# Gated pairs that take turns, retention states in one bank, and pauses in front of transpositions, in a two-layer hybrid decoder

## The chip, the cores and the metric

The kernel runs on one core of a Trainium2 chip. The metric is the device time of one execution in microseconds. The engines are named as the profile does: PE is TensorE (PEld its weight loads), DVE is VectorE, ACT is ScalarE, POOL is GpSimd, and SP issues the loads.

## What is computed

Two layers over 528 tokens (16 learned ones and 512 of the input) of width 1024, everything in float32. Each layer has a mixer and a gated feed-forward part. The mixer makes one projection to 3600 columns; four heads of retention and four heads of gated linear attention (GLA) work on it, and one output projection of 1024 columns follows. Cut to what matters here:

```python
def _mixer(h, pos, w_in, ...):
    rq, rk, rv, rg, gq, gk, gv, gr, ga = jnp.split(h @ w_in, offs, axis=-1)
    # retention: rotary on rq and rk, scores with a fixed decay per head, a state carried from chunk to chunk
    o_ret = _head_group_norm(_retention(rq, rk, rv), ret_norm_w) * silu(rg)
    # GLA: the decay of each key column is computed from the data (ga), a state carried likewise
    log_a = log_sigmoid(ga @ gla_gate_w2 + gla_gate_b) / GLA_TAU
    o_gla = _head_rms_norm(_gla(gq, gk, gv, log_a), gla_norm_w) * silu(gr)
    return jnp.concatenate([o_ret, o_gla], axis=-1) @ w_out

def _conv_ffn(h, ffn_up, ffn_conv_w, ffn_conv_b, ffn_down):
    u = h @ ffn_up                      # 2 x 2816 columns
    conv = ...                          # causal, depthwise, width 3
    a, g = jnp.split(conv, 2, axis=-1)
    return (gelu(a) * g) @ ffn_down

for i in range(2):
    h = h + _rmsnorm(_mixer(_rmsnorm(h, ...)), ...)
    h = h + _rmsnorm(_conv_ffn(_rmsnorm(h, ...)), ...)
```

## The kernel before

**Products.** Activations are kept transposed, with the 1024 columns on eight groups of 128 partitions and the 528 tokens along the free axis. Each float32 product is made of three float16 ones (`product_step`, L410 to L412): high part times high part, high times low, low times high. Weights come in blocks of 128 columns (`Block`), loaded by SP and split by ACT (L110) and DVE (L111) into a `unit`. A projection of one block is made in two halves of the tokens (232 and 296), 24 matmuls each, into the PSUM tile `pj`; its evacuation follows on ACT or, for the rotary heads, in `rope`.

**Work in the background.** The mixer's loop walks over the 29 blocks. After each half projection it calls `advance`, which gives one credit to each of two queues of Python generators and steps them while they have credit: `gated` holds the two GLA pairs (heads 0, 1 and heads 2, 3), `bg` all else. A plain step costs 0.6 of a credit, a step of a GLA level `LEVEL` of it. A generator that yields "waits" lets the next in its queue try. `pause(n)` yields "waits" until n further half projections have been made. So a generator's step decides where in program order its instructions come. The program order is a priority: a planner that knows estimated costs then orders each engine's instructions, and each engine keeps that order on the chip. The exception are parts marked to stay in program order. At the end of the mixer `drain` runs both queues until they are empty.

**GLA.** `gla(pr)` makes the decay (`gla_decay`), then `gla_scores`: a diagonal part and seven levels. At each level ACT and DVE write keys and queries as float16 pairs (`lvx`, L885 and L886), POOL and DVE multiply them by the decay for the level after (L888, L890), and in the following step `level_scores` makes the products (`lps`, L836), which DVE copies under a mask (L841 to L849). Then come `k_natural` (transpositions), `gla_states` (`kv`, L788 to L792) and, in a generator of its own in `bg`, `head_out`. In the queue `gated`, pair 0 is stepped to its end before pair 1.

**Retention.** `ret(hd)`: `ret_scores`, `k_natural`, `ret_states` (L775 and L776), `head_out`. In `ret_states` the four chunks are added up in one 128x128 part of a PSUM bank, which is copied after each:

```python
        ps = self.mx([P, P], "kv")
        for c in range(4):
            nc.tensor.matmul(ps, kn[:, c, :], vn(c), start=c == 0, stop=True, skip_group_check=c > 0)
            nc.scalar.activation(sn[:, c, :], ps, AF.Copy)
```

**Values and outputs.** `vtr` waits one half projection and transposes the values (`v_natural`, tile `ptv`). `head_out` multiplies scores and states with them (tile `o`, L694 to L701), normalises (retention: L712, L713, L724 on DVE; GLA: squares L719 and scaling L726 on ACT; the inverse roots on POOL, L344), waits for the gate, transposes the result (tile `pto`, L736), multiplies it by the gate (L739) and splits it into `merged` (L348, L349), from which the output projection (`po`) is made. All these PSUM tiles but those of the projections come from a pool of five banks (`mx`).

**Last feed-forward part.** In layer 1 the gated activations are written in quarters (`quarters`) for a product that needs seven products of quarter size in place of eight. Sums and early quarters lie in one tile `fk` for all eleven column groups.

## Time and profile before

| | |
|---|---|
| median of 3 runs | 1273.32 us (1272.81 to 1274.58) |
| the profiled execution | 1272.69 us, its span 1270.9 us |
| granted clock of PE, mean | 0.995 |
| busy: PE, PEld, DVE, ACT, POOL | 1236.3, 1018.6, 804.1, 666.0, 156.8 us |
| first matmul of the output projection, layer 0 and 1 | 244.51 us, 880.48 us |
| quarters' product in layer 1 | from 1159.40 us |

Times in the profile are counted from the span's start. The busy time of PE is that of overlapping matmuls with modelled ends, so it can be near the span while matmuls run slower than they might. The granted clock is the share of full speed that PE was given. In a row of a group, the numbers behind the first bar are busy time and mean nanoseconds of one; behind the second stands the idle time of the engine just before them, with what ended most of it. A wait goes by "who waited <- who released it".

### The profile page before, as it was taken

How to read it: one execution, taken by the hardware profiler on the slowest of the kernel's cores; microseconds unless marked ns; L12 is line 12 of the kernel's file. 1: busy time of each engine (PE TensorE's matmuls, PEld its weight loads, DVE VectorE, ACT ScalarE, POOL GpSimd, SP SyncE). 2: the span in 40 equal slices, each digit the busy share in tenths (PEclk: the TensorE clock that was granted, in tenths of full speed). 3: DMA queues.
4: the chain of work that ended last, by engine and by line, in shares of the span. 5: the costliest groups of instructions: out<-in, count | busy, mean ns of one | idle time of the engine just before them, and what ended most of it. 6: DMA issues, size and time to landing. Idle time of an engine off the chain costs nothing.

```text
span 1270.9 us, 26355 instructions
## 1 busy us (share of the span) xinstructions
PE 1236.3 (97%) x11106; PEld 1018.6 (80%) x11106; DVE 804.1 (63%) x1390; ACT 666.0 (52%) x1318; POOL 156.8 (12%) x206
## 2 busy tenths in 40 slices
PE   8999899999999999999999998999999999999997
PEld 7778678888788888888887786788898888886443
DVE  5584573557876666613286845735478867887677
ACT  5664554454855555523256645444547656664442
POOL 1021130044000000000141211310430000000001
PEclk9999999999999999999999999999999999999999
DMA  7832112222433333315142321122215333304471
GB/s 214 255 103 76 51 52 67 68 68 66 133 101 100 101 92 92 92 47 131 31 137 67 101 84 51 51 68 68 84 51 150 106 103 102 123 1 159 147 246 70
DMA packets 206827, 124.18 MB, mean 98 GB/s; under 512 B 6688, under 2 KB 194132, under 8 KB 206708
## 3 DMA queue, kind: packets, MB, share of 16 engines
q1 hardware_dynamic: 206548, 121.97, 32.4%
q8 instruction: 87, 1.43, 0.5%
q0 software_dynamic: 160, 0.52, 0.1%
q14 instruction: 32, 0.26, 0.1%
HBM read 120.38 MB, written 2.10 MB: 96 GB/s over the span
## 4 chain that ended last, share of the span: by engine, by line
PE 88%; DVE 5%; ACT 5%; POOL 1%; issue 1%; POOLq 0%; DVEq 0%; ACTq 0%
PE pu L411 12%; PE pu L412 12%; PE pu L410 12%; PE pl L1166 8%; PE pj L410 7%; PE pj L411 7%; PE pj L412 7%; PE pd L411 3%; PE pd L412 3%; PE pd L410 3%; PE po L411 2%; PE po L410 2%; PE po L412 2%; DVE unit L111 1%; ACT unit L110 1%; PE o L694 1%
## 5 line engine op out<-in xcount | busy, mean ns | idle before, releaser
L411 PE MATMUL pu<-every,unit 128*128 128x296 f16 (+2 forms) x1408 | 385.4, 274 | 2.1 <-DVE every L349 2.1
L412 PE MATMUL pu<-every,unit 128*128 128x296 f16 (+2 forms) x1408 | 385.4, 274 | 0.0
L410 PE MATMUL pu<-every,unit 128*128 128x296 f16 (+2 forms) x1408 | 383.7, 274 | 0.7 <-ACT every L348 0.7
L111 DVE SCALAR_TENSOR_TENSOR unit<-st,unit 128x1024 f16<-128x1024 f32 x184 | 229.1, 1246 | 191.1 <-ACT unit L110 190.6
L410 PEld LDWEIGHTS <-unit 128*128 128x128 f16 x2912 | 285.9, 98 | 50.6 <-issue 6.9
L412 PEld LDWEIGHTS <-unit 128*128 128x128 f16 x2912 | 285.8, 98 | 46.8 <-issue 3.1
L411 PEld LDWEIGHTS <-unit 128*128 128x128 f16 x2912 | 286.1, 98 | 42.6 <-issue 0.6
L110 ACT ACTIVATE unit<-st 128x1024 f16<-128x1024 f32 x184 | 191.4, 1041 | 121.3 <-PE pu L412 52.7
L410 PE MATMUL pj<-every,unit 128*128 128x296 f16 (+2 forms) x896 | 248.8, 278 | 1.3 <-DVE room L849 0.7
L412 PE MATMUL pj<-every,unit 128*128 128x296 f16 (+2 forms) x896 | 248.4, 278 | 0.7 <-DVE unit L111 0.7
L411 PE MATMUL pj<-every,unit 128*128 128x296 f16 (+2 forms) x896 | 248.5, 278 | 0.0
L1051 ACT ACTIVATE u<-pu 128x296 f32<-128x296 f32 (+2 forms) x176 | 66.4, 379 | 94.9 <-PE pu L412 94.8
L412 PE MATMUL pd<-av,unit 128*128 128x232 f16 (+1 forms) x352 | 96.9, 276 | 0.0
L411 PE MATMUL pd<-av,unit 128*128 128x296 f16 (+1 forms) x352 | 96.8, 276 | 0.0
L410 PE MATMUL pd<-av,unit 128*128 128x232 f16 (+1 forms) x352 | 96.7, 276 | 0.0
L376 DVE TENSOR_TENSOR acc<-acc,sq 128x296 f32<-128x296 f32 (+2 forms) x60 | 33.4, 558 | 81.5 <-ACT sq L374 79.6
L344 POOL TENSOR_TENSOR every<-every 128x1 f32<-128x1 f32 (+5 forms) x33 | 38.9, 1181 | 337.9 <-DVE every L343 169.5
L1166 PE MATMUL pl<-unit,fk 128*128 128x512 f16 x330 | 71.4, 379 | 0.0
L1040 DVE SCALAR_TENSOR_TENSOR cg<-u,every,cg 128x527 f32<-128x527 f32 (+1 forms) x88 | 66.7, 758 | 5.4 <-ACT cg L1035 4.3
L412 PE MATMUL po<-merged,unit 128*128 128x296 f16 (+2 forms) x256 | 70.0, 274 | 0.0
L411 PE MATMUL po<-merged,unit 128*128 128x296 f16 (+2 forms) x256 | 70.0, 274 | 0.0
L410 PE MATMUL po<-merged,unit 128*128 128x296 f16 (+2 forms) x256 | 69.6, 274 | 0.0
(224 smaller groups left out, 1515.7 us busy)
## 6 DMA issues: line engine op xcount, KB each, us to landing
st<-in_ffn_up SPq DMA_DIRECT2D x88, 512.0 KB, 3.7
st<-in_w_in SPq DMA_DIRECT2D x56, 512.0 KB, 4.5
st<-in_ffn_down SPq DMA_DIRECT2D x46, 512.0 KB, 3.8
st<-in_w_out SPq DMA_DIRECT2D x16, 512.0 KB, 3.5
st<-in_ffn_down SPq DMA_DIRECT2D x8, 384.0 KB, 3.0
out<-yo SPq DMA_DIRECT2D x8, 256.0 KB, 2.0
xt<-in_x SPq DMA_DIRECT2D x6, 256.0 KB, 6.5
w<-in_ffn_down SPq DMA_DIRECT2D x3, 512.0 KB
```

Of the source, the lines that this page charges most:

```text
L110: nc.scalar.activation(u[:, 0], st, AF.Copy, scale=SW)
L111: nc.vector.scalar_tensor_tensor(out=u[:, 1], in0=st, scalar=SW, in1=u[:, 0], op0=ALU.mult, op1=ALU.subtract)
L344: nc.gpsimd.tensor_tensor(out=r[:w, :n], in0=t[:w, :n], in1=self.mhalf[:w, :n], op=ALU.pow)
L376: eng.tensor_tensor(out=acc[:, :n], in0=acc[:, :n], in1=sq[:, :n], op=ALU.add)
L410: nc.tensor.matmul(ps[:, :n], w[:, 0, kk, :], x[:, 0, n0:n1], start=first, stop=False)
L411: nc.tensor.matmul(ps[:, :n], w[:, 0, kk, :], x[:, 1, n0:n1], start=False, stop=False)
L412: nc.tensor.matmul(ps[:, :n], w[:, 1, kk, :], x[:, 0, n0:n1], start=False, stop=last)
L694: nc.tensor.matmul(o[:, i, :], intra(i), vn(i), start=i == 0, stop=i == 0, skip_group_check=i > 0)
L1040: nc.vector.scalar_tensor_tensor(out=to, in0=u[:, max(lo, d) - d : L - d], scalar=self.cvec[:, ci(i) : ci(i) + 1], in1=to, op0=ALU.mult, o ...
L1051: nc.scalar.activation(u[:, n0:n1], ps[:, : n1 - n0], AF.Copy, scale=IXW)
L1166: mm = lambda x, w, **kw: nc.tensor.matmul(ps, x, w, skip_group_check=more, **kw)
```

## The change

There are five parts:

- Pairs: in the queue `gated` a generator that made a step goes to the end of the queue, so the two pairs alternate. `LEVEL` goes from 1.5 to 1.7. The ring of small value tiles `vnt` has eight places instead of six.
- Retention states: the four products go to four parts of one bank; ACT copies the first, DVE adds the others one after another. All is one step with a pause of two behind it.
- GLA states: one step instead of two, with a pause of two behind it and one of one in front.
- Pauses: two instead of one in front of `v_natural`, one in front of the retention states, two between normalisation and transpositions in `head_out`. There the two halves of a head come in one step instead of two. `drain` now counts beats, so that pauses end in it.
- The tile `fk` becomes eleven tiles, one for each column group.

```diff
-LEVEL = 1.5
+LEVEL = 1.7
...
-MIXKINDS = (("vnt", P, 6), ("mv", 10, 4), ...
+MIXKINDS = (("vnt", P, 8), ("mv", 10, 4), ...
...
                 if n != "waits":
+                    if queue is self.gated:
+                        queue.append(queue.pop(i))
                     return n or 1.0
...
     def drain(self):
         while self.bg or self.gated:
+            self.beat += 1
...
     def head_out(self, heads):
...
+        yield
+        yield from self.pause(2)
         for (on, ont), (*_, wcol, gate, slot, _) in zip(onvs, heads):
             while gate[0] is None:
                 yield "waits"
             merged = self.merged[slot] = self.g([P, 2, L], F16, "merged")
             for t0, t1, n0, n1 in [(0, 2, 0, HALF), (2, 5, HALF, L)]:
-                yield
                 pt = self.mx([P, WN], "pto")
...
                 self.split(merged, t[:, :w], n0, n1)
+            yield
...
     def ret_states(self, kn, vn, res):
-        ps = self.mx([P, P], "kv")
+        ps = self.mx([P, 4, P], "kv")
         for c in range(4):
-            nc.tensor.matmul(ps, kn[:, c, :], vn(c), start=c == 0, stop=True, skip_group_check=c > 0)
-            nc.scalar.activation(sn[:, c, :], ps, AF.Copy)
-            if c % 2:
-                yield
+            nc.tensor.matmul(ps[:, c, :], kn[:, c, :], vn(c), start=True, stop=True)
+        nc.scalar.activation(sn[:, 0, :], ps[:, 0, :], AF.Copy)
+        for c in range(1, 4):
+            nc.vector.tensor_tensor(out=sn[:, c, :], in0=sn[:, c - 1, :], in1=ps[:, c, :], op=ALU.add)
+        yield from self.pause(2)
...
     def gla_states(self, kn, tot, vn, res):
         nc.scalar.activation(sn[:, 0, :], ps[:, 0, :], AF.Copy)
-        yield
         for c in range(1, 4):
             nc.vector.scalar_tensor_tensor(out=sn[:, c, :], ...)
-        yield
+        yield from self.pause(2)
...
         def gla(pr):
             heads = (2 * pr, 2 * pr + 1)
+            yield from self.pause()
...
         def ret(hd):
             while ("rv", hd) not in vnat:
                 yield "waits"
+            yield from self.pause()
             yield from self.ret_states(res["kn"], vnat["rv", hd], res)
...
         def vtr(key):
-            yield from self.pause()
+            yield from self.pause(2)
...
         def quarters(col, ca, cg):
             if col == 0:
-                f = cell(self.keep, [P, 5, HK, HT], F32, "fk", "fk", 1)
...
             if col < HK:
-                f = keep["f"][:, j]
+                t = cell(self.keep, [P, 5 * HT], F32, "fk", "fk", HK)
+                f = t[:, : 3 * HT].rearrange("p (n t) -> p n t", n=3)
+                keep["f"].append(f)
+                keep["early"].append(...)
+                keep["sums"].append(...)
```

More of the change, by code (lines that the diff above doesn't have):

```diff
@@ L67 @@
 KINDS = (("rs_t", 10, 4), ("rs_r", 10, 4), ("sst", 1, 4))
-MIXKINDS = (("vnt", P, 6), ("mv", 10, 4), ("bst", 6, 8), ("ms", 10, 4), ("ont", P, 8), ("dgrt", 16, 4), ("dgt", 32, 2))
+MIXKINDS = (("vnt", P, 8), ("mv", 10, 4), ("bst", 6, 8), ("ms", 10, 4), ("ont", P, 8), ("dgrt", 16, 4), ("dgt", 32, 2))
 def cell(pool, shape, dt, tag, name, bufs=None):
@@ L1062, in quarters @@
             if col == 0:
-                f = cell(self.keep, [P, 5, HK, HT], F32, "fk", "fk", 1)
-                view = lambda t, n: t.rearrange("p n j t -> p (n j t)").rearrange("p (j n t) -> p j n t", j=HK, n=n)
-                keep.update(f=view(f[:, :3], 3), early=view(f[:, 3:].bitcast(F16), 4))
-                keep["sums"] = keep["f"].rearrange("p j n t -> p j (n t)").bitcast(F16).rearrange("p j (i n t) -> p j i n t", i=2, n=3)
-            if col == HK:
-                keep["late"] = self.room.bitcast(F16)[:, : HK * 4 * HT].rearrange("p (j n t) -> p j n t", j=HK, n=4)
-            if col < HK:
-                f = keep["f"][:, j]
+                keep["late"] = self.room.bitcast(F16)[:, : HK * 4 * HT].rearrange("p (j i n t) -> p j i n t", j=HK, i=2, n=2)
+                keep.update(f=[], early=[], sums=[])
+            if col < HK:
+                t = cell(self.keep, [P, 5 * HT], F32, "fk", "fk", HK)
+                f = t[:, : 3 * HT].rearrange("p (n t) -> p n t", n=3)
+                keep["f"].append(f)
+                keep["early"].append(t[:, 3 * HT :].bitcast(F16).rearrange("p (i n t) -> p i n t", i=2, n=2))
+                keep["sums"].append(t[:, : 3 * HT].bitcast(F16).rearrange("p (i n t) -> p i n t", i=2, n=3))
                 nc.vector.scalar_tensor_tensor(out=f[:, 0::2], in0=halves(ca), scalar=SA, in1=halves(cg), op0=ALU.mult, op1=ALU.mult)
@@ L1074, in quarters @@
             else:
-                f, e = cell(self.keep, [P, 5, HT], F32, "kl", "kl", 2), keep["f"][:, j]
+                f, e = cell(self.keep, [P, 5, HT], F32, "kl", "kl", 2), keep["f"][j]
                 nc.vector.scalar_tensor_tensor(out=f[:, :2], in0=halves(ca), scalar=SA, in1=halves(cg), op0=ALU.mult, op1=ALU.mult)
@@ L1081, in quarters @@
             for src, names, to in groups:
-                t = keep[to][:, j] if to == "sums" else keep[to][:, j].rearrange("p (i n) t -> p i n t", i=2)
+                t = keep[to][:, j] if to == "late" else keep[to][j]
                 nc.scalar.activation(t[:, 0], src, AF.Copy)
```

## The prediction

> **What bounds the kernel now.** I read the page first, then the stages, then what TensorE (PE) waited for, then the places where its clock fell. The page's span, busy shares and chain by engine:

> ```profile
> span 1270.9 us, 26355 instructions
> PE 1236.3 (97%) x11106; PEld 1018.6 (80%) x11106; DVE 804.1 (63%) x1390; ACT 666.0 (52%) x1318; POOL 156.8 (12%) x206
> PE 88%; DVE 5%; ACT 5%; POOL 1%; issue 1%; POOLq 0%; DVEq 0%; ACTq 0%
> ```

> PE sets the end: 88% of the chain. The number of its matmuls does not change, so only time in which PE waits or runs at a lower clock can be won. Where that is, the busy time by stage shows (stretch, its length, then PE, PEld, DVE, ACT, POOL busy, granted clock, DMA share, GB/s):

> ```profile
> 120.00:180.00 60.00, 55.24 (x588) 43.65 (x587) 40.55 (x108) 34.51 (x90) 15.54 (x17) 0.97 0.18 54
> 180.00:245.00 65.00, 64.27 (x583) 54.51 (x582) 28.68 (x72) 28.76 (x88) 5.50 (x5) 1.00 0.23 66
> 750.00:810.00 60.00, 54.03 (x555) 43.05 (x555) 37.27 (x101) 32.50 (x88) 12.59 (x17) 0.94 0.18 53
> 810.00:880.00 70.00, 69.33 (x667) 58.98 (x660) 34.02 (x84) 31.93 (x93) 8.44 (x14) 1.00 0.24 69
> 1110.00:1140.00 30.00, 30.00 (x274) 25.97 (x273) 25.49 (x37) 18.06 (x30) 0.00 (x0) 1.00 0.01 2
> ```

> The mixers lose 4.8 and 6.0 us in their middle, at 120:180 and 750:810, also with a lower clock; in the stretches after those PE lacks only 0.7 us each. The last feed-forward part (1110:1140) is full. The waits of PE, by who released it (total, times, longest):

> ```profile
> PE lps L836 <- ACT lvx L885: 2.4, 3, 1.1
> PE kv L775 <- ACT sn L776: 1.6, 3, 0.9
> PE pto L736 <- DVE on L724: 1.4, 2, 0.7
> PE ptv L661 <- ACT gv L923: 1.4, 1, 1.4
> PE lps L836 <- DVE lvx L886: 1.4, 3, 0.7
> PE pto L736 <- DVE tmp L739: 1.2, 2, 0.6
> PE pto L736 <- DVE room L849: 1.1, 2, 0.5
> PE kv L775 <- ACT room L670: 0.9, 2, 0.5
> PE lps L836 <- ACT merged L348: 0.7, 1, 0.7
> PE ptv L662 <- ACT vn L669: 0.6, 2, 0.3
> PE lps L836 <- DVE tmp L739: 0.4, 1, 0.4
> ```

> These are what the edits aim at: level scores (lps) whose operand was just being made, states (kv) alternating with ScalarE's copies, transpositions (pto, ptv) issued right behind what they transpose. One such place, in order of time (start, duration, instruction, in brackets the idle time before):

> ```profile
> 155.52 0.41 PE L736 MATMUL pto<-every,on 128*128 128x128 f32 x2 [0.54 <-DVE room L849]
> 155.82 0.91 DVE L739 SCALAR_TENSOR_TENSOR tmp<-pto,every,gr 128x256 f32<-128x256 f32 x2
> 156.62 1.38 DVE L724 TENSOR_SCALAR on<-o,room,every 128x128 f32<-128x128 f32 x4
> 156.78 0.19 PE L836 MATMUL lps<-lvx 64*128 64x64 f16 x1 [0.44 <-DVE tmp L739]
> 158.05 0.46 PE L736 MATMUL pto<-every,on 128*128 128x128 f32 x2 [0.72 <-DVE on L724]
> ```

> Outputs of a gated pair, normalisation of a retention head and a level meet on VectorE (DVE), and PE, which keeps its order, waits 1.7 us in three pieces. What follows such a place, in stretches of 3.4 us (columns as above):

> ```profile
> 155.10:158.50 3.40, 1.76 (x10) 0.93 (x10) 3.40 (x12) 0.84 (x2) 0.87 (x1) 0.98 0.00 0
> 158.50:161.90 3.40, 3.40 (x16) 2.15 (x16) 3.40 (x10) 1.86 (x5) 1.79 (x2) 0.52 0.00 0
> 790.00:793.40 3.40, 1.64 (x10) 1.05 (x10) 3.40 (x13) 0.84 (x2) 0.82 (x1) 0.97 0.02 4
> 793.40:796.80 3.40, 3.40 (x16) 2.10 (x17) 3.40 (x10) 1.90 (x5) 1.90 (x2) 0.52 0.02 5
> 803.40:806.80 3.40, 3.40 (x21) 2.73 (x19) 3.40 (x11) 2.40 (x4) 0.68 (x2) 0.51 0.03 7
> 702.00:705.40 3.40, 1.58 (x12) 1.13 (x13) 2.43 (x5) 1.24 (x2) 0.00 (x0) 1.00 0.23 66
> ```

> After a stretch with PE busy for about half, 3.4 us run at half clock: three times, each worth 3.4 x (1 - 0.52) = 1.6 us, 4.9 in all. It is no sure consequence: 702.0 was as empty and the clock stayed.

> **The change, part by part.** I count places in slots, one after each half projection (0 to 57 in a layer), by following the credits: 1 per slot, a plain step costs 0.6, a level 1.5 before and 1.7 after.

> *Turns and LEVEL.* Before, pair 0 has its levels at slots 15, 16, 18, 19, 21, 22, 24, 25 and pair 1 at 31 to 42. After, pair 0 at 17, 21, 24, 27, 31, 34, 38, 41 and pair 1 at 19, 22, 26, 29, 33, 36, 39, 43. The density is nearly the same, but between the preparation of a level and its scores lie 3.3 slots instead of 1.5. That should end the waits of lps for lvx: 2.4 + 1.4 = 3.8 us. Instructions: none added. Moved: pair 0's states from slot 27 to 47 and the products of its output from 30 to 49, and its output transpositions from 33-35 to 52. So the place at 155 us loses one of its three parties, and the late stretch (180:245), where DVE has 36 us free of 65, gets it. More tiles live at once (my count: 26 instead of 20 of 41 slots), so nothing waits for a slot. The longer ring of small v tiles (8 for 6) is needed, because the first gated one is now held to slot 49 and the seventh is made at 45: no wait either. No DMA is issued by the moved steps, so SP's queue keeps its order; POOL's powers and level products move with their steps and POOL is busy 5.5 of 65 us there.

> *Retention states.* Four products go into four parts of a bank instead of one that is copied and added to in turn, one copy and three adds follow. The prices come from these groups:

> ```profile
> L776 ACT ACTIVATE sn<-kv 128x128 f32<-128x128 f32 x32 | 8.8, 274 | 28.6 <-PE kv L775 28.6
> L792 DVE SCALAR_TENSOR_TENSOR sn<-sn,tots,kv 128x128 f32<-128x128 f32 x12 | 4.1, 345 | 12.0 <-ACT sn L789 11.8
> ```

> ```profile
> DVE sn L792 <- ACT sn L789: 11.8, 4, 3.0
> ```

> Over 8 heads ACT loses 24 x 0.274 = 6.6 us, DVE gains 24 adds; the form (a plain add from PSUM) is not in the trace, its nearest is L792, so 24 x 0.345 = 8.3 us. Both lie beside PE: DVE is 63% busy. PE's wait for the copies, 1.6 us, goes. A new wait is DVE's for the first copy: the same step of the gated pairs has DVE wait 11.8 us in four, 3.0 at most, so at most 8 x 3.0 = 24 us, behind which rope and weight splits queue. No wait row of PE names those four, so I take 0; the pause of two slots behind the adds (48 matmuls) covers their 0.27 + 3 x 0.35 = 1.3 us. If the cover goes, it is 1.3 x 8 = 10 us, the other end; below zero it cannot go by more than the 1.6 already counted.

> *Pauses.* A pause is no wait on the chip: it moves the step one or two slots back in program order. In front of v transpositions and states it should take the 1.4 (ptv behind gv) and the 0.9 (kv behind L670). In front of output transpositions: 1.4 + 1.1, and the 0.7 and 0.4 that level scores waited in the same crowd, 3.6 in all. I leave standing 1.2 (pto behind tmp) and 0.6 (ptv behind vn): those wait for a PSUM bank, and the two halves of a head are now issued in one step, which helps no bank. Who waits for a later output? The output projection alone, whose last operand is the head of the last gate (slot 57) before and after.

> *Eleven tiles.* The same operations on the same number of bytes, in separate tiles. The largest of them:

> ```profile
> L1084 DVE TENSOR_TENSOR fk<-kl,fk 128x768 f16<-128x768 f32 x11 | 10.5, 956 | 6.4 <-ACT fk L1083 6.4
> ```

> PE is full there and DVE has 4.5 of 30 us free. The cost lies between 0 and one such split that comes late, 1.0 us; a gain is excluded, since PE has nothing to win in 1110:1140. I take 0. The added beat in the last drain only lets pauses end.

> *Sum.* Waits 3.8 + 1.6 + 1.4 + 0.9 + 3.6 = 11.3. Clock: the three crowds thin out, but 702.0 shows that it hangs on more than the filling; I take two of three, 3.3. Against it, new waits in slots 44 to 57, where both pairs' states and outputs now lie together: between 0 and what states and outputs cost today (1.6 + 1.4 + 0.9 + 3.6 = 7.5); I take the middle, 4, since the free DVE speaks for less and the doubled halves for more. 11.3 + 3.3 - 4 = 10.6. The profiled execution took 1272.69, so 1262.1; the median of the runs stands 0.6 above it: 1263.

> [...]

> **The rivals.**
> (E) More comes back than I count: all three clock stretches, no new wait, and the refill behind each wait. The flow of matmuls shows the refill:

> ```profile
> 130.20 0.26 PE L412 MATMUL pj<-every,unit 128*128 128x232 f16 x1
> 130.30 0.26 PE L410 MATMUL pj<-every,unit 128*128 128x232 f16 x1
> ```

> They start 0.10 apart and last 0.26, so a wait loses 0.16 beyond its bracket; 18 waits make 2.9. 11.3 + 4.9 + 2.9 = 19.1: 1254.

> (B) The waits only move. The planner orders PE by its own estimates, and every reshuffle has places where they are wrong. Then only the 1.6 of the states and little else goes: 1271. For it: the waits sit at different places in the two layers. Against: the releasers are the same few, and all get more distance.

> [...]

> (D) Slower: PSUM banks. Five banks serve all but the projections; a pair's output takes four from its products until it is scaled. Its rows:

> ```profile
> L726 ACT ACTIVATE on<-o,every 128x128 f32<-128x128 f32 x32 | 8.9, 356 | 2.2 <-POOL every L344 2.2
> L719 ACT ACTIVATE on<-o 128x128 f32<-128x128 f32 x32 | 8.3, 276 | 19.0 <-PE o L699 19.0
> L719 ACT ACTIVATION_READ_ACCUMULATOR on<-o 128x1 f32 x32 | 6.7, 208 | 0.0
> L344 POOL TENSOR_TENSOR every<-every 128x1 f32<-128x1 f32 (+5 forms) x33 | 38.9, 1181 | 337.9 <-DVE every L343 169.5
> ```

> Ten squares of 0.276 + 0.208, a power of 1.2, ten scalings of 0.356: 9.6 us. The pairs now come at slots 49 and 50, and retention heads between. If PE waits out one pair's hold in each layer, 19.2, and one clock stretch each, 3.2, against 11.3 + 3.3 gained, it is 7.8 slower: 1281. It decides from 7.3 us of such waits a layer. For it: bank waits exist (1.2, 0.6). Against: slots 44 to 57 hold fourteen half projections that the planner can put in between, and pair 1's output there costs PE almost nothing today (0.7 us idle in 180:245).

> **How the numbers follow.** Forecast 0.60 (1257 to 1269, 1263 its middle), E 0.10, B 0.12, C 0.06, D 0.12. The range leaves out D and the slow end of C: 1253 to 1275. About 0.2%, 2.5 us, is what a measurement of this kernel tells from no change. Faster: forecast, E and a twentieth of the rest, 0.75; same: B and part of C, 0.12; slower: D and the rest of C, 0.13.

> **What would show it.** Level scores with no wait for lvx; kv with no wait for sn; PE fuller in 120:180 and 750:810 and the clock at 1.00 there; in the late stretches more DVE and ACT work, and up to 4 us of waits of pto and o. The last feed-forward part unchanged. Wrong it would be if those late stretches lose more than they did in the middle, or if half clock appears behind the transpositions at slots 47 to 55.

## The result, and the profile after

The changed kernel takes 1250.37 us (median of 4 runs, 1250.15 to 1251.25) against 1273.28 us for the kernel before: a ratio of 0.982, with an interval of 0.9803 to 0.9837. It is 22.9 us faster, more than twice the forecast of 10.3 and below the low end of the range. Its profiled execution has a span of 1248.4 us, 22.5 less.

Page and chain of the changed kernel:

```profile
span 1248.4 us, 26366 instructions
PE 1227.0 (98%) x11106; PEld 1017.4 (81%) x11106; DVE 806.5 (65%) x1414; ACT 654.2 (52%) x1290; POOL 157.1 (13%) x206
PE 92%; DVE 3%; POOL 2%; ACT 1%; issue 1%; DVEq 0%; POOLq 0%; ACTq 0%
```

As many matmuls as before, 24 instructions more on DVE and 28 fewer on ACT. 24 of these are copies of the states. The other four are ACT_TABLE_LOADs of 1.28 us each, which I had not foreseen: the decays of both pairs now run in turns, and each of two lines has one load in a layer where it had two (groups of the kernel before, then of the changed one):

```profile
L819 ACT ACT_TABLE_LOAD x4 | 5.1, 1283 | 0.1
L923 ACT ACT_TABLE_LOAD x4 | 5.1, 1283 | 0.1
```

```profile
L824 ACT ACT_TABLE_LOAD x2 | 2.6, 1283 | 0.0
L928 ACT ACT_TABLE_LOAD x2 | 2.6, 1283 | 0.0
```

PE is a still larger part of the chain. The stages that answer to those shown of before (stretch, length, PE, PEld, DVE, ACT, POOL busy, clock, DMA share, GB/s):

```profile
120.00:180.00 60.00, 60.00 (x693) 51.59 (x692) 38.69 (x100) 26.99 (x55) 12.48 (x16) 1.00 0.28 80
180.00:236.00 56.00, 55.33 (x488) 46.56 (x486) 28.02 (x82) 28.66 (x107) 6.24 (x4) 1.00 0.17 48
740.00:800.00 60.00, 60.00 (x720) 51.30 (x719) 40.35 (x104) 26.76 (x55) 13.69 (x23) 1.00 0.25 73
800.00:858.00 58.00, 57.37 (x509) 48.17 (x507) 27.77 (x81) 29.91 (x109) 6.51 (x8) 1.00 0.19 55
1090.00:1120.00 30.00, 30.00 (x278) 26.25 (x276) 25.55 (x36) 19.02 (x31) 0.00 (x0) 1.00 0.01 1
```

The middle of both mixers is full, where 4.8 and 6.0 us were missing, and the clock is 1.00. In the late stretches PE lacks 0.7 and 0.6 us, no more than before, though both pairs' states and outputs now lie there. The last feed-forward part is unchanged. The stretch in which PE was busy for 1.76 of 3.40 us before is full now, with the same DVE at its limit:

```profile
155.10:158.50 3.40, 3.40 (x51) 2.77 (x49) 3.40 (x7) 1.06 (x1) 2.07 (x3) 1.00 0.34 101
```

What is left of PE's waits in the mixers, but for 0.8 us of pj in front of the levels (total, times, longest):

```profile
PE pto L740 <- DVE on L727: 1.0, 2, 0.7
PE d L871 <- DVE dg L873: 0.9, 1, 0.9
PE ptv L665 <- DVE dg L873: 0.6, 1, 0.6
PE pto L740 <- DVE tmp L743: 0.3, 1, 0.3
```

No lps and no kv is in the list. The slack has changed sides: now DVE sits idle for 16.1 us until level scores come, 8 times; before, that was 2.5 us in 3 (first row of the changed kernel, second of the kernel before, from what the users of the tile lps waited for):

```profile
  PE lps L841: 16.1, 8
  PE lps L836: 2.5, 3
```

By the first matmul of each stage, the 22.5 us split as follows: layer 0 from the gate logits (z) to the first product of the output projection took 205.9 us and takes 195.7; layer 1 from the first projection to there, 226.5 and 213.0; the opening, which the change does not touch, is 1.2 us longer (over all profiles of this document the first gate logits come between 38.6 and 40.3 us); all the rest is the same within 0.2. So 10.1 and 13.5 come from the two mixers and from nowhere else.

### The profile page after: what moved, and what is told of

It reads as the page before. It is cut to its first block, busy times and chain, and to the rows that moved or that the text cites. A ratio compares the mean times of both kernels' runs of the same rounds, so it can differ in the third digit from the quotient of the medians.

```text
span 1248.4 us, 26366 instructions
## 1 busy us (share of the span) xinstructions
PE 1227.0 (98%) x11106; PEld 1017.4 (81%) x11106; DVE 806.5 (65%) x1414; ACT 654.2 (52%) x1290; POOL 157.1 (13%) x206
## 4 chain that ended last, share of the span: by engine, by line
PE 92%; DVE 3%; POOL 2%; ACT 1%; issue 1%; DVEq 0%; POOLq 0%; ACTq 0%
PE pu L414 12%; PE pu L415 12%; PE pu L413 12%; PE pl L1173 8%; PE pj L413 8%; PE pj L415 7%; PE pj L414 7%; PE pd L413 3%; PE pd L414 3%; PE pd L415 3%; PE po L413 2%; PE po L415 2%; PE po L414 2%; PE lps L841 1%; DVE unit L111 1%
## 5 line engine op out<-in xcount | busy, mean ns | idle before, releaser
L111 DVE SCALAR_TENSOR_TENSOR unit<-st,unit 128x1024 f16<-128x1024 f32 x184 | 227.1, 1234 | 162.0 <-ACT unit L110 156.3
L347 POOL TENSOR_TENSOR every<-every 128x1 f32<-128x1 f32 (+5 forms) x33 | 38.9, 1181 | 289.2 <-DVE every L346 192.0
```

The source lines that it names most:

```text
L111: nc.vector.scalar_tensor_tensor(out=u[:, 1], in0=st, scalar=SW, in1=u[:, 0], op0=ALU.mult, op1=ALU.subtract)
L347: nc.gpsimd.tensor_tensor(out=r[:w, :n], in0=t[:w, :n], in1=self.mhalf[:w, :n], op=ALU.pow)
```

## The experiments

Twelve kernels ran, each five rounds or more against the kernel before on the same chip; numbers are ratios to that. e1 to e4 shared one chip, e5 to e8 a second, e9 to e12 a third. The changed kernel itself has 0.982 in the result and 0.9801 as e9 and did not run beside e5 to e8, so distances to it are given for both. I began with three theories. Theory 1, distance: each wait of PE costs its bracket, a refill and now and then 3.4 us at half clock, and the parts take waits away by putting steps farther behind their operands. Theory 2, place: the gain is that pair 0's output leaves the crowded middle. Theory 3: a lucky reshuffle. After the first four runs I added theory 4: the parts need one another.

**Each part alone.** e1 has the turns:

```diff
-LEVEL = 1.5
+LEVEL = 1.7
-... ("vnt", P, 6) ...
+... ("vnt", P, 8) ...
...
                 if n != "waits":
+                    if queue is self.gated:
+                        queue.append(queue.pop(i))
```

> The kernel before with the turns, LEVEL 1.7 and the longer ring of small value tiles alone. Theory 1 (distance: a wait of PE costs its bracket, a refill and now and then 3.4 us at half clock; turns take the waits of lps for lvx, 3.8 us, the pair's part in the crowds at 155 and 790, 2.2 us, two or three clock stretches, 3.3 to 4.9, and refills, 2): 11 to 13 us faster than before, about 1261. Theory 2 (place: nearly all of the gain comes from moving pair 0's output out of the crowded middle): 18 us or more faster, 1255 or less. Theory 3 (a lucky reshuffle of the planner's order, parts do not add): between 3 faster and 3 slower, with new waits at other places.

Measured: 0.996 (0.9948 to 0.9973), 5 us, less than half of what I expected. The waits of lps for lvx are gone, as I had said, but others came (PE's waits in e1):

```profile
PE kv L777 <- ACT vn L671: 2.5, 2, 1.2
PE pto L738 <- ACT on L728: 2.3, 3, 1.9
PE lps L838 <- DVE on L726: 2.2, 2, 1.1
PE ptv L663 <- ACT gv L925: 2.0, 1, 2.0
```

All but one are behind ACT. And the clock fell where it had not before, at the end of layer 1 (stages of e1):

```profile
858.00:862.00 4.00, 1.87 (x13) 1.11 (x12) 0.83 (x2) 2.02 (x9) 2.00 (x2) 1.00 0.44 131
862.00:866.00 4.00, 4.00 (x17) 3.20 (x18) 3.56 (x10) 2.67 (x10) 0.11 (x1) 0.54 0.02 4
866.00:870.00 4.00, 4.00 (x17) 3.55 (x18) 0.44 (x1) 1.46 (x9) 0.00 (x0) 0.50 0.00 0
870.00:874.00 4.00, 4.00 (x20) 2.23 (x20) 0.17 (x1) 1.84 (x13) 0.79 (x1) 0.50 0.01 2
874.00:878.00 4.00, 4.00 (x29) 2.92 (x27) 0.00 (x0) 0.64 (x2) 1.16 (x1) 0.76 0.00 0
```

This stretch of half clock lasts 13.7 us, and 6.8 are lost. The profiled run took 1270.78 us; six of the twelve runs of e1 take 1266.2 to 1267.4 at a higher mean clock (0.992 to 0.995 against 0.990), so its row in the table below has more half clock than they. Theory 2 falls with e1: pair 0's output is out of the middle and most of the gain is not there.

e2 has the pauses and merged steps alone: two beats instead of one in front of the values, one in front of states, two behind those of the gated pairs, and these lines in the outputs:

```diff
+        yield
+        yield from self.pause(2)
         for (on, ont), (*_, wcol, gate, slot, _) in zip(onvs, heads):
...
             for t0, t1, n0, n1 in [(0, 2, 0, HALF), (2, 5, HALF, L)]:
-                yield
                 pt = self.mx([P, WN], "pto")
```

> The kernel before with the pauses and the merged steps alone (values, states, outputs), queues and states' arithmetic as before. Theory 1: the waits of pto, ptv L661 and kv behind L670 go, 3.6 + 1.4 + 0.9 us, with two clock stretches, 3.3, and refills, 1.6: about 11 us faster, 1262; lps still waits for lvx. Theory 2: at most 4 us faster, because pair 0's output stays in the middle. Theory 3: within 3 us, new waits elsewhere.

Measured: 0.9984 (0.9975 to 0.9992), 2 us. The waits of pto shrank to 0.4, and lps still waited for lvx (2.9 of the 3.8 before). New ones stood at other places, pj behind DVE rk for 2.2 and behind ACT gv for 1.8, which is what theory 3 had said of this run.

e3 has the states alone:

```diff
-        ps = self.mx([P, P], "kv")
+        ps = self.mx([P, 4, P], "kv")
...
+        nc.scalar.activation(sn[:, 0, :], ps[:, 0, :], AF.Copy)
+        for c in range(1, 4):
+            nc.vector.tensor_tensor(out=sn[:, c, :], in0=sn[:, c - 1, :], in1=ps[:, c, :], op=ALU.add)
...
```

> The kernel before with the retention states in four parts of a bank and DVE adds alone, no pause. Theory 1: kv no longer waits for sn, 1.6 us plus three refills of 0.16: 2 us faster, 1271; 24 adds of about 0.35 us appear on DVE. Theory 2: the same 2 us. Theory 3: within 3 us of before either way.

Measured: 0.9942 (0.993 to 0.9954), 7 us, three times what the wait of kv for sn was worth. That wait went, another wait of kv came (3.0 behind ACT on), and yet PE's brackets over both mixers fell by 3.9 us in all and the half clock by 1.7 (table below): waits changed at many places, not only at the states. The profiled run took 1268.78 us; three of the other four take 1265.7 to 1266.2 with a mean clock of 0.998, as high as that of the changed kernel. e4 has the eleven tiles alone, the last hunk of the diff:

> The kernel before with the eleven tiles alone. All theories: no difference, 1273 within 1.5 us; waits of PE and the clock stretches as before. If it is more than 3 us faster, the tiles give the mixer room that I did not count.

Measured: 1.0004 (0.9995 to 1.0012). Nothing, as said. The single tile together with the other parts was not tried.

Alone, the parts give 5, 2, 7 and 0 us; together 23. So they do not add up, and the next question was which need which.

**One part taken out of the changed kernel.** e5 has the pairs one after the other (without the two lines in the queue, LEVEL 1.7 kept):

> The changed kernel with the pairs one after the other again (LEVEL 1.7, states, pauses and tiles as changed). Parts that add up (theory 1, turns alone gave 0.4%, 5 us): 1255 to 1256. Parts that need one another (theory 4: turns, states and pauses each take one cause of the same crowds, and waits and half clock go only when the crowd goes): 1260 to 1264, with waits of lps for lvx and at least one half-clock stretch per layer. Theory 2 (place of pair 0's output): as theory 4 or worse, 1265.

Measured: 0.9866 (0.9851 to 0.9881), 6 to 8 us slower than the changed kernel. Waits of lps for lvx are back and the clock falls with them (waits of PE, then three stretches of e5):

```profile
PE lps L839 <- ACT lvx L888: 3.9, 2, 2.0
PE lps L839 <- DVE lvx L889: 2.1, 2, 1.1
```

```profile
157.00:160.40 3.40, 1.55 (x37) 1.09 (x35) 3.40 (x8) 0.79 (x2) 0.80 (x1) 1.00 0.30 90
160.40:163.80 3.40, 2.30 (x11) 1.45 (x12) 3.40 (x12) 2.91 (x8) 0.00 (x0) 0.51 0.22 65
163.80:167.20 3.40, 3.40 (x16) 2.10 (x14) 2.19 (x6) 1.03 (x3) 2.96 (x3) 0.50 0.00 0
```

That is 6.8 us of half clock in each layer. PE waits through the first 1.0 and 1.8 us of it, so it is worth some 2.9 and 2.5 us. Output transpositions stand right in front (156.3 to 157.7 and 785.1 to 786.4 us), then level scores and the two waits, so this run does not part the waits from the transpositions as the cause (the last section has a half clock without any). e6 has the old copies in the states:

```diff
-        ps = self.mx([P, 4, P], "kv")
+        ps = self.mx([P, P], "kv")
         for c in range(4):
-            nc.tensor.matmul(ps[:, c, :], kn[:, c, :], vn(c), start=True, stop=True)
-        nc.scalar.activation(sn[:, 0, :], ps[:, 0, :], AF.Copy)
-        for c in range(1, 4):
-            nc.vector.tensor_tensor(out=sn[:, c, :], in0=sn[:, c - 1, :], in1=ps[:, c, :], op=ALU.add)
+            nc.tensor.matmul(ps, kn[:, c, :], vn(c), start=c == 0, stop=True, skip_group_check=c > 0)
+            nc.scalar.activation(sn[:, c, :], ps, AF.Copy)
```

> The changed kernel with the retention states as before, four products and four copies in turn, in one step. By the waits of kv for sn alone: 2 us slower than the changed kernel, 1252. By what the states gave when changed alone (0.6%, 7 to 8 us): 1258. Theory 4 says 1254 to 1258, with waits of kv for sn and half clock behind them.

Measured: 0.9837 (0.9823 to 0.9851), 2 to 5 us slower by the ratios, and no half clock in the mixers. That is not the wait that I had named: PE never waits for sn here. Its brackets are 1.7 us longer than in the changed kernel, and the new ones are o and pj behind DVE tmp (1.0 and 0.8). e7 is without the output pause, with the halves of a head in two steps (`yield` in front of each):

> The changed kernel without the pause between normalisation and output transpositions, and with the halves of a head in two steps again. Parts that add up: at most 2 us slower, 1250 to 1253. Theory 4: waits of pto for DVE on come back, 3 us and one or two clock stretches, 1254 to 1258.

Measured: 0.9799 (0.9785 to 0.9813). Nothing is lost, and pto does not wait at all. The part to which I gave 3.6 us of waits is worth nothing once the others are in. e8 has LEVEL 1.9:

> The changed kernel with LEVEL 1.9 for 1.7: pairs end some three slots later. Distance (theory 1): nothing left to win for lps, within 2 us of 1250. If the late stretch (states and outputs of both pairs) is near its limit: 3 us or more slower, with waits of pto and o.

Measured: 0.9807 (0.9792 to 0.9821), no difference from 0.982. The late stretch is not near a limit.

**Pairs of parts, and the yardstick.** e9 is the changed kernel again, on the chip of the last three:

> The changed kernel once more, as the yardstick for the kernels beside it. All theories: 0.982 of before within 0.0015, no half clock inside the mixers, waits of PE there below 4 us in all.

Measured: 0.9801 (0.9787 to 0.9814). e10 has turns, states and tiles, no pause:

> The kernel before with turns, LEVEL 1.7, the longer ring, the eleven tiles and the new retention states, and no pause at all. Parts that add up (turns 0.4%, states 0.6%): 12 to 13 us faster than before, 0.990. Theory 4 (pauses in front of values and states are the third condition): 0.989 to 0.992, with waits of ptv and kv behind ACT and half clock. If pauses do nothing but cost: 0.982 to 0.984, the changed kernel's time.

Measured: 0.9832 (0.9818 to 0.9845). That is 21 us of the 25 that the changed kernel has on this chip, from parts that give 5 and 7 alone. The waits of kv behind L671 that e1 had are gone with the copies; two of ptv stay (waits of PE in e10):

```profile
PE ptv L663 <- ACT gv L927: 2.0, 1, 2.0
PE ptv L663 <- ACT vn L666: 1.2, 1, 1.2
```

e11 is the changed kernel with only the output pause and that of the retention states:

> The changed kernel without the pauses in front of values and in front of and behind the states of both kinds except that of the new retention states; output pauses kept. Theory 4: the waits of ptv for gv (2.0) and kv for L671 (2.5), which the turns alone had, come back with half clock: 5 to 8 us slower than the changed kernel, 0.986 to 0.988. If these pauses are as idle as the output pause: within 2 us of it.

Measured: 0.9837 (0.985 at most, 0.9823 at least), 4.6 us slower than e9. The waits of ptv are back, in the same amounts as in e10; in both kernels 1.7 us of the loss are a stretch of half clock at 647 us, between the layers, where PE waits in every kernel. e12 puts e7 and e8 together:

> The changed kernel without the output pause (as in e7) and with LEVEL 1.9 (as in e8), which were 0.2% and 0.1% faster than 0.982 each, at the edge of their intervals. If both are real and add up: 0.979, 3 to 4 us faster than the changed kernel. If each only took the same last waits (pto for DVE, 1.3 us): 0.980. If it is a reshuffle: 0.980 to 0.983.

Measured: 0.9814 (0.9801 to 0.9827). No gain over the changed kernel; e12 has a stretch of half clock between the layers that e9 has not.

Of the three parts that act, this is the whole table (ratio to before; e5 with LEVEL 1.7):

| | neither | states | pauses | both |
|---|---|---|---|---|
| pairs in sequence | 1 | 0.9942 | 0.9984 | 0.9866 |
| pairs in turns | 0.996 | 0.9832 | 0.9837 | 0.982, 0.9801 |

One part gives 0.2 to 0.6%, any two 1.3 to 1.7%, the third 0.1 to 0.7% more: any two give more than their sum, and the third no more than about what it gives alone. Only in that weak form do the parts need one another. What theory 4 had foretold came in part: e5 has the waits of lps and the half clock in each layer. But e5 (1257.78 against 1260 to 1264), e7 (1249.15 against 1254 to 1258) and e10 (0.9832 against 0.989 to 0.992) are faster than it said, e11 (0.9837) lies between both answers, and e6 (1254.14) meets its 1254 to 1258 without the waits and the half clock that were to cause it. Theory 1 is left for how a wait is priced. For that I took two stretches of each of the fourteen profiles, from the gate logits to the first feed-forward product, and added up PE's bracketed waits and the time lost to a lower clock, over both layers. It is one profiled execution of each kernel, and the clock is taken at its full price, which is too much where PE waits meanwhile (e5, e2):

| kernel | length, us | waits, us (number) | lost to the clock, us | the rest, us |
|---|---|---|---|---|
| before | 498.8 | 16.4 (30) | 5.1 | 477.2 |
| e4 tiles | 500.2 | 16.7 (29) | 6.8 | 476.7 |
| e3 states | 492.6 | 12.5 (20) | 3.4 | 476.6 |
| e2 pauses | 497.9 | 12.2 (15) | 5.1 | 480.6 |
| e1 turns | 495.9 | 11.9 (14) | 10.3 | 473.7 |
| e5 no turns | 483.4 | 9.4 (10) | 6.8 | 467.3 |
| e6 old states | 478.2 | 5.2 (10) | 0 | 473.0 |
| e10, e11 | 477.6, 478.4 | 4.5 (6) | 0 | 473.1, 473.9 |
| after | 475.1 | 3.5 (7) | 0 | 471.6 |
| e7 | 474.0 | 3.2 (6) | 0 | 470.8 |

The six profiles with 9.4 us of waits and more have half clock there, those with 5.2 and less have none (e8, e9 and e12, not in the table, have 2.4 to 3.6 and none). That may be a part of why two parts give more than their sum: one part alone (e1, e2, e3) left 11.9 to 12.5 us of waits, and half clock with them. Within the mixers waits and half clock are shown only as going together; no run changed one without the other. But it is no sure consequence, as the mean clock of 0.998 in three runs of e3 suggests, and the last section shows the same waits, between the layers, with and without it. A fit of the 28 lengths with a base for each layer and the lost clock at its full price gives 1.11 us for each microsecond of bracket and 0.18 us for each wait, with 1.3 us left unexplained in a stretch. Length and number of the waits go together, so the fit hardly parts them (standard errors 0.26 and 0.16; with brackets alone it gives 1.37, with 1.4 unexplained); that 0.18 is near the refill of 0.16 proves nothing.

## Why the prediction was right or wrong

**Right: what bounds the kernel and where.** Only PE's waits and clock in the mixers could be won, and all of it came from there, 10.1 and 13.5 us. The last feed-forward part and the tiles gave 0, as said (e4: 1.0004). The waits named went: lps for lvx, kv for sn and for L670, ptv for gv; pto behind DVE fell from 2.5 (on and room) to 1.0. That is most of the 11.3 foretold. The brackets over the two stretches fell from 16.41 to 3.46, by 13.0, since most of those that I left standing went too (pto behind tmp 1.2, now 0.3).

**Right: no cost on DVE.** I took 24 adds at 0.345 and a wait of DVE for the first copy of at most 24 us. The adds took 0.279 each, DVE's wait was 11.2 us, and PE named neither (groups and waits of the changed kernel):

```profile
L783 DVE TENSOR_TENSOR sn<-sn,kv 128x128 f32<-128x128 f32 x24 | 6.7, 279 | 11.4 <-ACT sn L781 11.2
DVE sn L783 <- ACT sn L781: 11.2, 4, 3.2
```

**Wrong: the new waits.** The sum was 10.6 and the mixers gave 23.7. Of the 13.1 that are missing, the brackets are 5.7, the clock 1.8 and what the sum left out 5.6. The term in the sum that failed most is "new waits in slots 44 to 57 ... I take the middle, 4". Pto waits there for 1.3 us in the changed kernel, and PE lacks 1.3 us in both late stretches together, as many as before. The lower end, 0, was right. I let "the doubled halves" speak for more against a row that said less: 36 us of free DVE time.

**Wrong: the clock.** "I take two of three, 3.3": all three went, 5.1 us by the granted clock. The row that made me cautious, 702.0, showed one stretch with 1.82 of 3.40 us idle and the clock still at 1.00 behind it, not that the half clock of the others would stay. How much of it there is, is partly luck: it is one profile of each kernel, and the mean clock differs between runs of one program (0.989 to 0.995 in e1, 0.993 to 0.998 in e3).

**Wrong: the refill left out of the sum.** I had it, 0.16 for each wait, and put it into rival E alone. Beyond brackets and clock the length lost 5.6. The starts of the matmuls give an estimate of what that is (against the median distance of the same shape to the next one, without bracket and at full clock, over all profiles): the first matmuls behind brackets were late by another 5.0 us before and are by 1.2 now, so 3.8 for 23 waits, 0.16 each. Nearly all that is left, some 2 us, lies where PE goes from one kind of matmul to another without a bracket, 299 times before and 247 now.

With these three the sum is 13.0 + 5.1 + 5.6 = 23.7, less 1.2 of a longer opening 22.5; the 5.6 is the remainder, so this sum closes by construction. That is rival E (19.1, chance 0.10) and more. Rivals B and D fell: few waits moved, and PE waits 1.5 us for DVE's copies of dg (d and ptv), far from the 19.2 of D. C, with 0.06 of the chances, is the case that half clock appears behind the output transpositions: it did not, ten of them at 222.4 to 224.2 us left the clock at 1.00. But all three were near: e2 is B (0.9984, waits at new places), and what turns cost without new states (e1) is a stall behind both pairs' late outputs, though it was ACT's work and not the banks that PE waited for, with a half clock that begins at 862.3 us inside a lump of transpositions. That these were its cause no run shows, and that of e12 came without any (last section).

**Wrong: the shares of the edits.** By edits the account fails too. I gave the output pause 3.6 us of waits and it is worth nothing in the changed kernel (e7); I gave the states 1.6 and alone they give 7 (e3); the turns' 3.8 of lps show as 6 to 8 when they are taken out (e5) and 5 when they come alone. My explanation is that a wait does not belong to one edit: three parties met at 155 us, and taking out any one of them thins the crowd. No run shows that directly.

What stays open: the table's rest differs by up to 13 us between kernels (e5 467.3, e2 480.6) without a bracket that shows it; waits shorter than the modelled end of the matmul before them would not show. Open is why the clock stayed up in some crowds and not in others. Open too is how the planner's order turns one edit into gains at places far from it, as in e3.

## What to carry to other kernels

When one engine is the bound and a few short waits are spread over a stage, sum them with their refill and with the clock that may fall behind them, not by brackets alone: here brackets of 13.0 us went together with 3.8 of refill and 5.1 of clock, and 23.7 were gained. Changes that thin the same crowd are not additive, so judge each by taking it out of the best version as well as by putting it into the old one: the output pause was free to drop, and turns and states gave 21 us together but 5 and 7 alone. Work that leaves a crowded stage is best moved to where the other engines have idle time in the windows view (36 us of 65 on DVE here), and the forecast should charge new waits there only where a row shows that engine to be near its limit.

## What the runs showed of the hardware

```profile
642.04:645.45 3.41, 1.67 (x14) 1.22 (x12) 3.40 (x6) 2.16 (x6) 0.34 (x8) 1.00 0.29 70
645.45:648.86 3.41, 2.90 (x31) 2.86 (x30) 3.41 (x11) 1.94 (x7) 0.00 (x0) 1.00 1.13 312
642.37:645.78 3.41, 1.15 (x11) 0.76 (x9) 3.40 (x9) 2.84 (x7) 0.35 (x8) 1.00 0.55 150
645.78:649.20 3.42, 3.42 (x20) 2.62 (x18) 3.42 (x11) 1.53 (x4) 0.00 (x0) 0.50 1.18 302
```

In the changed kernel the brackets lie in two pieces, 1.74 us idle in the first, and the clock stays at 1.00; in e12 2.26 us fall into one piece, and the next runs at 0.50. PE did nothing but projections and feed-forward products in that piece of e12, so this half clock came without transpositions and without level scores.

Half clock did not always end after 3.41 us: it held for 13.7 us in e1 (862.3 to 875.9), while PE always had work, until 872.4 transpositions and the small products of the outputs, then projections. In e5 it held for 6.8 us in each layer, with PE waiting at the start; no bracket of PE in e5 is over 2.0 us. In such a stretch 128x296 products started 0.25 us apart instead of 0.13, as in the kernel before from 158.9 us on and, at full clock again, from 161.8 (start, duration, instruction):

```profile
158.88 0.45 PE L411 MATMUL pj<-every,unit 128*128 128x296 f16 x1
159.12 0.45 PE L412 MATMUL pj<-every,unit 128*128 128x296 f16 x1
161.80 0.29 PE L411 MATMUL pj<-every,unit 128*128 128x296 f16 x1
161.93 0.29 PE L412 MATMUL pj<-every,unit 128*128 128x296 f16 x1
```

It also goes with an uneven time: the runs of e1 lie in two groups, 1266.2 to 1267.4 us with a mean clock of 0.992 to 0.995 and 1270.8 to 1272.7 with 0.989 to 0.990, those of the changed kernel within 1.1 us.
